# The first norm of a decoder layer: three token blocks ahead of any split, the other six in two groups of three

## The chip, the cores and the metric

The kernel runs on one core of a Trainium2 chip. The metric is the device time of one execution in microseconds. A core has a matrix engine (TensorE, PE in the rows, with its weight loads as PEld), a vector engine (VectorE, DVE), a scalar engine for activations, copies and casts (ScalarE, ACT), GpSimd (POOL), and SyncE (SP), which here issues DMA transfers. Each engine takes its instructions in order and waits on semaphores for the others.

## The reference

One step of a hybrid decoder layer for 1056 tokens (1024 of a prompt and 32 of eight samples) of width 1024, in float32. Cut to what the change touches:

```python
def _rmsnorm(x, g):
    y = x * lax.rsqrt(jnp.mean(x * x, axis=-1, keepdims=True) + EPS) * g
    return y

h = _rmsnorm(x, norm1)
z = h @ w_in                     # columns: hq, hf, hi, hog, aq, ak, av, iq, ik, iw, ga, gb
hq, hf, hi, hog, aq, ak, av, iq, ik, iw, ga, gb = jnp.split(z, offs, axis=-1)
# HGRN2 recurrence over hq, hf, hi; its output is normed and multiplied with silu(hog)
# sparse attention over aq, ak, av with an indexer iq, ik, iw
# merge with sigmoid(ga), sigmoid(gb), projection w_o, residual
# second norm, squared-ReLU MLP, residual, final norm
```

## The kernel before

The kernel is one program of some 31,000 instructions. It is written as a sequence of tile operations, and the build (`schedule_with_timeline_sim=True`, near the end of the file) plans the order on each engine from a simulated timeline: among instructions that are ready the one that stands earlier in the text goes first, and those written under `tc.high_priority()` go ahead of others. So the text sets which work is preferred, and data dependencies set what can't be overtaken.

**Split products.** A float32 product is made of three: each operand is split into a high part, rounded to the type `F32R`, and a low part, the rest. The high part is a cast on ScalarE, the low part a subtraction on VectorE. `wload` (L142 to L150) loads 128 columns of a weight matrix (512 KB) from SyncE into the raw tile `wr`, of which there is one buffer, and splits it into `wh` and `wl`, of which there are two each. In `wload` the split has high priority. `gemm3` (L152) does the three products for each of eight pieces of 128 rows, and `proj` and `proj_two` run it over three column pieces of 352 tokens (`CUTS`), so that the first piece needs token blocks 0 to 2, the second blocks 2 to 5, the third blocks 5 to 8.

**The first norm** (L208 to L240). Tokens come in nine blocks of 128 (the last has 32). `GROUPS` takes them as 0, 1, 2, (3, 4), (5, 6), (7, 8). For a group:

- each block is loaded (`xt`, SyncE) and squared with a row sum into `ss` (L225, ScalarE);
- `rstd_of` (L183) makes 1/sqrt: a step on VectorE (L186), a square root on ScalarE (L187), a reciprocal and three small steps on VectorE (L188 to L192);
- for each block the product `ht` = x * rstd * g (L234, VectorE), eight transposes on TensorE into a two-bank tile of PSUM (L238; `ps_s` has two buffers), the high split `hh` (L239, ScalarE) and the low split `hl` (L240, VectorE), both of which read that tile.

Once the group that holds block 2 (`FIRST_W`) is squared, the first two weight tiles are loaded: `whi` (input) and `whog` (output gate) of head 0. After the last group its rstd gives `zc` (L244) and from it `idr`, an identity matrix, with which the raw tokens are transposed too (`xTp`, L253, TensorE), copied (L255) and stored for the residual. These transposes and the later work are free to be planned among the products.

**After it** comes the loop over four heads of the HGRN2 branch (L393). For head 0 the products `whi` and `whog` run piece by piece in turn (`proj_two`, L406): `ev_i` copies, `ev_og` (L396) takes the sigmoid of the gate on ScalarE and multiplies. Square root and sigmoid use different tables of ScalarE, and going from one to the other shows as an ACT_TABLE_LOAD.

Of the kernel before, what the change touches and what calls it, by code (L numbers as in the profile page):

```python
# [10 lines left out]
F32 = mybir.dt.float32  # L11
# [3 lines left out]
AF = mybir.ActivationFunctionType  # L15
ALU = mybir.AluOpType
# [3 lines left out]
D = 1024  # L20
# [15 lines left out]
N_UNITS = 26  # L36
DOTS_S, DOTS_L = "sstts", "sstsstss"
CUTS = (0, 352, 704, 1056)

GROUPS, FIRST_W = ((0,), (1,), (2,), (3, 4), (5, 6), (7, 8)), 2  # L40

TH, TC = 528, 264
ORDER = ("P1", "P2", "P6", "P5", "P7", "P4", "P3")
# [18 lines left out]
C_HQ, C_HF, C_HI, C_HOG, C_AQ, C_AK, C_AV, C_IQ, C_IK, C_GA, C_GB = (  # L62
    0, 512, 1024, 1536, 2048, 2560, 3072, 3584, 4096, 4168, 5192)
# [37 lines left out]
def hybrid_step(ctx: ExitStack, tc, x_prompt, x_sample, cache_k, cache_v, cache_idx_k, state_hgrn,  # L101
# [3 lines left out]
    nc = tc.nc  # L105
    dbg = dbg or {}

    cst = ctx.enter_context(tc.tile_pool(name="cst", bufs=1))
# [30 lines left out]
    hl = big.tile([128, 8, T], F32R, name="hl", tag="hl")  # L139


    def wload(rows, c0, nk, m, name):  # L142
        raw = wp.tile([128, nk, m], F32, name=name + "r", tag="wr", bufs=1)
        nc.sync.dma_start(raw, rows[:, c0:c0 + m].rearrange("(k p) m -> p k m", p=128))
        wh = wp.tile([128, nk, m], F32R, name=name + "h", tag="wh", bufs=2)
        wl = wp.tile([128, nk, m], F32R, name=name + "l", tag="wl", bufs=2)
        with tc.high_priority():
            nc.scalar.copy(wh, raw)
            nc.vector.tensor_tensor(wl, raw, wh.bitcast(F32), op=ALU.subtract)
        return wh, wl  # L150

# [49 lines left out]
    g1 = U.get([128, 1024], F32, "g1")  # L201
    nc.scalar.dma_start(g1, bass.AP(tensor=norm1.tensor, offset=norm1.offset, ap=[[0, 128], [1, D]]))

    def tok(tb):
        n = 128 if tb < 8 else NS
        return n, slice(tb * 128, tb * 128 + n)
# [3 lines left out]
    nc.scalar.activation(zc, ones[:, 0:1], AF.Sqrt)  # L210
    hr = Ring(U, 6)
    xts = []
    first_w = None
    for grp in GROUPS:
        ss = sm.tile([128, 3], F32, name="ssx", tag="ssx", bufs=3)
        if 8 in grp:
            nc.vector.memset(ss, 1.0)
        hts = []
        for a, tb in enumerate(grp):
            n, cs = tok(tb)  # L220
            xt = U.get([128, 1024], F32, "xt")
            src = x_prompt[0, cs, :] if tb < 8 else x_sample.rearrange("s q d -> (s q) d")
            nc.sync.dma_start(xt[:n], src)
            ht = hr.get([128, 1024], F32, "ht")
            nc.scalar.activation(ht[:n], xt[:n], AF.Square, accum_out=ss[:n, a:a + 1])  # L225
            xts.append(xt)
            hts.append(ht)
        if not first_w and grp[-1] >= FIRST_W:
            first_w = [wload(w_in[0], C_HI, 8, 128, "whi"), wload(w_in[0], C_HOG, 8, 128, "whog")]
        rs = rstd_of(ss[:, :len(grp)], len(grp), 1.0 / D, "rsx")  # L230
        for a, tb in enumerate(grp):
            n, cs = tok(tb)
            ht = hts[a]
            nc.vector.scalar_tensor_tensor(ht[:n], xts[tb][:n], rs[:n, a:a + 1], g1[:n], op0=ALU.mult, op1=ALU.mult)  # L234
            pst = ps_s("hTp")
            pv = pst.rearrange("p a (b c) -> p (a b) c", c=128)
            for k in range(8):
                nc.tensor.transpose(pv[:, k, :n], ht[:n, k * 128:(k + 1) * 128], ident[:n, :n])  # L238
            nc.scalar.copy(hh[:, :, cs], pv[:, :, :n])  # L239
            nc.vector.tensor_tensor(hl[:, :, cs], pv[:, :, :n], hh[:, :, cs].bitcast(F32), op=ALU.subtract)  # L240
    U.put(g1)
    hr.close()

# [149 lines left out]
    for h in range(4):  # L393
        vT = U.get([128, T], F32, "vT")

        def ev_og(ps, sl, c):  # L396
            sg_ = sm.tile([128, CH], F32, name="sgo", tag="c352", bufs=2)
            sg_ = sg_[:, :sl.stop - sl.start]
            nc.scalar.activation(sg_, ps, AF.Sigmoid)
            nc.vector.tensor_tensor(sil[:, sl], ps, sg_, op=ALU.mult)  # L400

        def ev_i(ps, sl, c):
# [1134 lines left out]
```

## Time and profile before

| | us |
|---|---|
| median of 3 runs | 1807.02 |
| the three runs | 1801.29, 1807.02, 1813.28 |
| the profiled execution | 1804.69 |
| its span, first to last instruction | 1803.0 |
| TensorE busy in the span | 1718.2 |
| VectorE busy | 1222.6 |
| ScalarE busy | 867.4 |

The profile is one execution taken by the hardware profiler. A timeline row has the start and the length of an instruction (or of several alike, "x8"), its engine, line, operation, output tile and inputs, and in brackets how long the engine was idle before it and which instruction it then waited for. A row of stretches has how long each engine was busy in a stretch. Matmuls overlap, so that the spacing of their starts says more than the length of one.

### The profile page before, as it was taken

To read this page: it belongs to the slowest core of one execution; us is meant where nothing else is said; L and a number is where in the kernel's file an instruction comes from. 1 tells how busy PE (TensorE), PEld (TensorE's weight loads), DVE (VectorE), ACT (ScalarE), POOL (GpSimd) and SP (SyncE) were. 2 spreads that over 40 slices of the span, in tenths; PEclk is the share of its full clock that TensorE was granted. 3 is DMA by queue.
4 is the path that set the end of the run, shared out by engine and by line. 5 is a ranking of instruction groups with operands and counts; after the bars stand their busy time and mean duration, and the time that the engine had idled before them with its cause. 6 is when DMAs were issued, how large, how long until landed. Compare 5 with 4: busy or idle time off the path is not lost.

```text
span 1803.0 us, 30879 instructions
## 1 busy us (share of the span) xinstructions
PE 1718.2 (95%) x11980; PEld 1656.2 (92%) x11980; DVE 1222.6 (68%) x2767; ACT 867.4 (48%) x1645; POOL 216.7 (12%) x244
## 2 busy tenths in 40 slices
PE   6999999999999999979999999999999999999887
PEld 6999999999999998877899998999999899999867
DVE  7275585745799897965747569777677866566535
ACT  6456465334578833234724455444344644444412
POOL 1100000023000015740100230000000000000110
PEclk9999999999999999999999999999999999999998
DMA  5411111231223234552543243444334877676763
GB/s 167 132 49 48 49 56 48 61 94 34 84 68 96 77 95 130 172 180 66 162 143 108 95 132 99 145 151 160 132 132 156 275 178 182 174 185 166 171 155 115
DMA packets 162706, 221.92 MB, mean 123 GB/s; under 512 B 12096, under 2 KB 117856, under 8 KB 162560
## 3 DMA queue, kind: packets, MB, share of 16 engines
q1 hardware_dynamic: 137472, 148.60, 26.4%
q0 software_dynamic: 18032, 62.18, 13.4%
q10 hardware_dynamic: 7056, 9.18, 1.4%
q8 instruction: 94, 1.54, 0.4%
q14 instruction: 52, 0.43, 0.1%
HBM read 140.31 MB, written 76.77 MB: 120 GB/s over the span
## 4 chain that ended last, share of the span: by engine, by line
PE 38%; DMA 9%; issue 8%; DVE 4%; ACT 3%; POOL 2%; DVEq 0%; SPq 0%; POOLq 0%; ACTq 0%
PE pua L1336 13%; PE puc L1336 7%; PE pub L1336 3%; DMA qb<-q_d 2%; PE po L158 2%; PE po L157 2%; PE po L156 2%; DMA h2a<-hc_d 2%; DMA wdr<-in_w_down_dram 1%; POOL qb L924 1%; DMA h2b<-hc_d 1%; DMA wbsg<-sg_d 1%; DVE pr L923 1%; PE wbp L156 1%; PE wbp L157 1%
## 5 line engine op out<-in xcount | busy, mean ns | idle before, releaser
L1336 PE MATMUL pua<-h2P,wP 128*128 128x264 f32 x1248 | 196.1, 285 | 3.5 <-ACT uu L1398 3.1
L1336 PE MATMUL pua<-h2a,wP 128*128 128x264 f32 x960 | 161.7, 287 | 13.6 <-ACT uu L1398 10.6
L1336 PEld LDWEIGHTS pua<-h2P,wP 128*128 128x128 f32 x1248 | 170.4, 189 | 4.5 <-ACT uu L1398 4.0
L1336 PEld LDWEIGHTS pua<-h2a,wP 128*128 128x128 f32 x960 | 134.6, 189 | 18.9 <-ACT uu L1398 14.8
L1398 ACT COPY uu<-pua 128x264 f32<-128x264 f32 x192 | 72.0, 378 | 133.5 <-PE pua L1336 127.4
L156 PE MATMUL wgt<-hh,wgth 128*128 128x352 f32 x384 | 126.1, 328 | 0.0
L158 PE MATMUL wgt<-hh,wgtl 128*128 128x352 f32 x384 | 125.1, 326 | 0.0
L157 PE MATMUL wgt<-hl,wgth 128*128 128x352 f32 x384 | 124.6, 324 | 0.0
L1336 PE MATMUL pua<-h2b,wP 128*128 128x264 f32 x672 | 118.4, 285 | 0.0
L1336 PE MATMUL puc<-h2P,wP 128*128 128x264 f32 x720 | 111.0, 284 | 0.6 <-DVE hd L1402 0.6
L1440 POOL DMA_DIRECT2D x_d<-hd x32 | 27.9, 873 | 612.6 <-ACT wP L1302 359.5
L1336 PEld LDWEIGHTS puc<-h2P,wP 128*128 128x128 f32 x720 | 97.1, 188 | 0.8 <-DVE hd L1402 0.8
L777 ACT ACTIVATE jkA<-sc,bstg 128x1024 bf16<-128x1024 bf16 (+5 forms) x93 | 87.1, 936 | 21.3 <-DVE bstg L796 6.0
L1336 PEld LDWEIGHTS pua<-h2b,wP 128*128 128x128 f32 x672 | 96.8, 189 | 0.1
L772 DVE TENSOR_SCALAR_CACHE_REDUCE jkD<-sc,bstg 128x768 bf16<-128x768 f32 (+3 forms) x96 | 84.4, 879 | 0.9
L1303 DVE TENSOR_TENSOR wP<-w1r,wP 128x512 fp32r<-128x512 f32 (+2 forms) x96 | 62.8, 655 | 28.8 <-ACT wP L1302 28.0
L1302 ACT CAST wP<-w1r 128x512 fp32r<-128x512 f32 (+2 forms) x96 | 57.0, 595 | 46.7 <-PE puc L1336 28.1
L156 PEld LDWEIGHTS wgt<-hh,wgth 128*128 128x128 f32 x384 | 72.2, 188 | 2.0 <-issue 1.0
L157 PEld LDWEIGHTS wgt<-hl,wgth 128*128 128x128 f32 x384 | 72.2, 188 | 1.2 <-issue 0.5
L158 PEld LDWEIGHTS wgt<-hh,wgtl 128*128 128x128 f32 x384 | 72.2, 188 | 1.2 <-issue 0.6
L1336 PE MATMUL puc<-h2a,wP 128*128 128x264 f32 x384 | 70.6, 286 | 0.9 <-DVE hd L1408 0.9
L158 PE MATMUL po<-mh,wol 128*128 128x352 f32 x192 | 62.2, 324 | 0.0
(788 smaller groups left out, 5071.2 us busy)
## 6 DMA issues: line engine op xcount, KB each, us to landing
x_d<-hd POOLq DMA_DIRECT2D x32, 528.0 KB
hc_d<-hd SPq DMA_DIRECT2D x56, 264.0 KB, 2.8
h2P<-hc_d SPq DMA_DIRECT2D x45, 264.0 KB, 3.7
sg_d<-gst ACTq DMA_DIRECT2D x48, 176.0 KB, 2.0
h2a<-hc_d SPq DMA_DIRECT2D x32, 264.0 KB, 2.8
wgtr<-in_w_in_dram SPq DMA_DIRECT2D x16, 512.0 KB, 3.9
qb<-q_d POOLq DMA_DIRECT2D x16, 512.0 KB
w1r<-in_w_up_dram SPq DMA_DIRECT2D x16, 512.0 KB, 3.9
```

The costliest lines, as they stand in the source:

```text
L156: nc.tensor.matmul(ps, wh, xh, start=(k == 0), stop=False)
L157: nc.tensor.matmul(ps, wh, xl, start=False, stop=False)
L158: nc.tensor.matmul(ps, wl, xh, start=False, stop=(k == n - 1))
L772: nc.vector.tensor_scalar(jkD[:, 0, :L], SC[i], s if isinstance(s, float) else s[:, a:a + 1], 0.0, op0=op, op1=ALU.add, accum_out=out[:, a ...
L777: nc.scalar.activation(jkA[:, 0, :(i + 1) * 128], src(i), AF.Sign, bias=thr[:, a:a + 1], accum_out=cnt[:, a:a + 1])
L923: nc.vector.tensor_tensor(pr, kp[:, 0:1, :].to_broadcast([128, 2, 512]), qb, op=ALU.mult)
L924: nc.gpsimd.tensor_tensor(qb, kp[:, 1:2, :].to_broadcast([128, 2, 512]), qb, op=ALU.mult)
L1302: nc.scalar.copy(w[:, 0, :n], src)
L1303: nc.vector.tensor_tensor(w[:, 1, :n], src, w[:, 0, :n].bitcast(F32), op=ALU.subtract)
L1336: nc.tensor.matmul(ps, w[:, a, k], x[:, b, sl], start=(q in "P1P2P5" and k == n_ == 0), stop=(k == k1 - k0 - 1 and n_ == 2), skip_group_ch ...
L1398: nc.scalar.copy(uu[c][:, {"P1": u1, "P6": 1, "P7": 2}[q]], ps)
L1440: nc.gpsimd.dma_start(x1_d[2 * i + e], hd[j][e], accum_op=ALU.add)
```

## The change

The first three blocks are normed (`norm`) one by one, before any of them is transposed and split (`turn`). A column of ones, `one`, is computed from the rstd of block 2 (the maximum with 1, then the minimum with 1, is 1 for every number) and is the scale with which ScalarE writes the high splits of blocks 0 and 1 and of the `whi` weights; these therefore follow the third root. The other six blocks go in two groups of three. The second group's factor `inv` (1/1024 for every number) is computed from a column of the high split of block 3, so that its root follows that split. The splits of the first two weights have no high priority any more; `whi` is loaded after block 0 is turned and `whog` after blocks 3 to 5 are normed. The scale `onel`, a one from the last group's rstd, makes the first sigmoid follow the last root. In `wload` the cast of the high part, for all weights, is written as an activation (Copy with a scale) instead of a copy.

```diff
--- before.py
+++ after.py
@@ -37,8 +37,6 @@
 DOTS_S, DOTS_L = "sstts", "sstsstss"
 CUTS = (0, 352, 704, 1056)
 
-GROUPS, FIRST_W = ((0,), (1,), (2,), (3, 4), (5, 6), (7, 8)), 2
-
 TH, TC = 528, 264
 ORDER = ("P1", "P2", "P6", "P5", "P7", "P4", "P3")
 
@@ -139,13 +137,13 @@
     hl = big.tile([128, 8, T], F32R, name="hl", tag="hl")
 
 
-    def wload(rows, c0, nk, m, name):
+    def wload(rows, c0, nk, m, name, late=None):
         raw = wp.tile([128, nk, m], F32, name=name + "r", tag="wr", bufs=1)
         nc.sync.dma_start(raw, rows[:, c0:c0 + m].rearrange("(k p) m -> p k m", p=128))
         wh = wp.tile([128, nk, m], F32R, name=name + "h", tag="wh", bufs=2)
         wl = wp.tile([128, nk, m], F32R, name=name + "l", tag="wl", bufs=2)
-        with tc.high_priority():
-            nc.scalar.copy(wh, raw)
+        with tc.high_priority() if late is None else ExitStack():
+            nc.scalar.activation(wh, raw, AF.Copy, scale=1.0 if late is None else late)
             nc.vector.tensor_tensor(wl, raw, wh.bitcast(F32), op=ALU.subtract)
         return wh, wl
 
@@ -210,8 +208,9 @@
     nc.scalar.activation(zc, ones[:, 0:1], AF.Sqrt)
     hr = Ring(U, 6)
     xts = []
-    first_w = None
-    for grp in GROUPS:
+
+    def norm(grp, inv=1.0 / D):
+
         ss = sm.tile([128, 3], F32, name="ssx", tag="ssx", bufs=3)
         if 8 in grp:
             nc.vector.memset(ss, 1.0)
@@ -225,19 +224,47 @@
             nc.scalar.activation(ht[:n], xt[:n], AF.Square, accum_out=ss[:n, a:a + 1])
             xts.append(xt)
             hts.append(ht)
-        if not first_w and grp[-1] >= FIRST_W:
-            first_w = [wload(w_in[0], C_HI, 8, 128, "whi"), wload(w_in[0], C_HOG, 8, 128, "whog")]
-        rs = rstd_of(ss[:, :len(grp)], len(grp), 1.0 / D, "rsx")
+        rs = rstd_of(ss[:, :len(grp)], len(grp), inv, "rsx")
         for a, tb in enumerate(grp):
             n, cs = tok(tb)
-            ht = hts[a]
-            nc.vector.scalar_tensor_tensor(ht[:n], xts[tb][:n], rs[:n, a:a + 1], g1[:n], op0=ALU.mult, op1=ALU.mult)
+            nc.vector.scalar_tensor_tensor(hts[a][:n], xts[tb][:n], rs[:n, a:a + 1], g1[:n], op0=ALU.mult,
+                                           op1=ALU.mult)
+        return grp, hts, rs
+
+    def turn(grp, hts, rs):
+
+        for ht, tb in zip(hts, grp):
+            n, cs = tok(tb)
             pst = ps_s("hTp")
             pv = pst.rearrange("p a (b c) -> p (a b) c", c=128)
             for k in range(8):
                 nc.tensor.transpose(pv[:, k, :n], ht[:n, k * 128:(k + 1) * 128], ident[:n, :n])
-            nc.scalar.copy(hh[:, :, cs], pv[:, :, :n])
+            nc.scalar.activation(hh[:, :, cs], pv[:, :, :n], AF.Copy, scale=one[:, 0:1] if tb < 2 else 1.0)
             nc.vector.tensor_tensor(hl[:, :, cs], pv[:, :, :n], hh[:, :, cs].bitcast(F32), op=ALU.subtract)
+
+
+    normed = [norm((tb,)) for tb in range(3)]
+
+    one = cst.tile([128, 1], F32, name="one")
+    nc.vector.tensor_scalar(one, normed[2][2][:, 0:1], 1.0, 1.0, op0=ALU.max, op1=ALU.min)
+    turn(*normed[0])
+    first_w = [wload(w_in[0], C_HI, 8, 128, "whi", late=one)]
+    turn(*normed[1])
+    turn(*normed[2])
+    inv = 1.0 / D
+    for grp in ((3, 4, 5), (6, 7, 8)):
+        normed = norm(grp, inv)
+        if len(first_w) == 1:
+            first_w.append(wload(w_in[0], C_HOG, 8, 128, "whog", late=1.0))
+        turn(*normed)
+
+        inv = cst.tile([128, 1], F32, name=f"inv{grp[0]}")
+        nc.vector.tensor_scalar(inv, hh[:, 7, tok(grp[0])[1]][:, 127:128].bitcast(F32), 1.0 / D, 1.0 / D,
+                                op0=ALU.max, op1=ALU.min)
+    rs = normed[2]
+
+    onel = cst.tile([128, 1], F32, name="onel")
+    nc.vector.tensor_scalar(onel, rs[:, 0:1], 1.0, 1.0, op0=ALU.max, op1=ALU.min)
     U.put(g1)
     hr.close()
 
@@ -396,7 +423,7 @@
         def ev_og(ps, sl, c):
             sg_ = sm.tile([128, CH], F32, name="sgo", tag="c352", bufs=2)
             sg_ = sg_[:, :sl.stop - sl.start]
-            nc.scalar.activation(sg_, ps, AF.Sigmoid)
+            nc.scalar.activation(sg_, ps, AF.Sigmoid, scale=onel if h == c == 0 else 1.0)
             nc.vector.tensor_tensor(sil[:, sl], ps, sg_, op=ALU.mult)
 
         def ev_i(ps, sl, c):
```

## Rows read from the trace of the kernel before

**Rows 1.** The page's busy times: us, share of the span, instructions.
```profile
PE 1718.2 (95%) x11980; PEld 1656.2 (92%) x11980; DVE 1222.6 (68%) x2767; ACT 867.4 (48%) x1645; POOL 216.7 (12%) x244
```

**Rows 2.** Busy times by stretches: length, engines, granted clock (PEclk), DMA share, GB/s.
```profile
0.00:50.00 50.00, 34.44 (x219) 32.75 (x220) 33.66 (x123) 32.40 (x54) 9.61 (x24) 1.00 0.52 164
...
800.00:850.00 50.00, 39.94 (x216) 29.99 (x215) 22.84 (x77) 20.13 (x39) 3.13 (x6) 0.90 0.22 68
```

**Rows 3.** The same view, of a stretch soon after the start.
```profile
25.40:30.40 5.00, 5.00 (x34) 5.00 (x32) 4.89 (x9) 1.02 (x1) 0.00 (x0) 1.00 0.38 103
```

**Rows 4.** TensorE's timeline of the start: start, length, line, operation, count [idle before].
```profile
9.87 1.94 PE L238 MATMUL hTp<-ident,ht 128*128 128x128 f32 x8 [9.87 <-DVE rsx L186]
...
18.44 1.94 PE L238 MATMUL hTp<-ident,ht 128*128 128x128 f32 x8 [4.30 <-DVE rsx L186]
...
21.40 1.94 PE L238 MATMUL hTp<-ident,ht 128*128 128x128 f32 x8 [1.02 <-DVE ht L234]
...
25.62 0.32 PE L158 MATMUL whi<-hh,whil 128*128 128x352 f32 x1
...
25.77 0.32 PE L156 MATMUL whi<-hh,whih 128*128 128x352 f32 x1
...
34.54 1.04 PE L253 MATMUL xTp<-idr,xt 128*128 128x128 f32 x8
...
36.65 0.41 PE L156 MATMUL whi<-hh,whih 128*128 128x352 f32 x1
```

**Rows 5.** ScalarE's timeline of the start.
```profile
9.93 1.04 ACT L225 ACTIVATE ht<-xt 128x1024 f32<-128x1024 f32 x1
...
11.84 1.01 ACT L239 CAST hh<-hTp 128x1024 fp32r<-128x1024 f32 x1 [0.78 <-PE hTp L238]
...
12.75 1.05 ACT L148 CAST whih<-whir 128x1024 fp32r<-128x1024 f32 x1
...
13.70 0.20 ACT L187 ACTIVATE rsx<-rsx 128x1 f32<-128x1 f32 x1
...
24.29 0.21 ACT L187 ACTIVATE rsx<-rsx 128x2 f32<-128x2 f32 x1
...
33.58 1.28 ACT L399 ACT_TABLE_LOAD   x1
...
34.88 0.46 ACT L399 ACTIVATE sgo<-whog 128x352 f32<-128x352 f32 x1
```

**Rows 6.** VectorE's timeline of the start.
```profile
10.05 0.16 DVE L188 RECIPROCAL rsx<-rsx 128x1 f32<-128x1 f32 x1 [0.27 <-ACT rsx L187]
...
10.83 1.28 DVE L234 SCALAR_TENSOR_TENSOR ht<-xt,rsx,g 128x1024 f32<-128x1024 f32 x1
...
12.03 0.15 DVE L186 TENSOR_SCALAR rsx<-ssx 128x1 f32<-128x1 f32 x1
...
14.03 1.22 DVE L149 TENSOR_TENSOR whil<-whir,whih 128x1024 fp32r<-128x1024 f32 x1
...
17.01 1.28 DVE L234 SCALAR_TENSOR_TENSOR ht<-xt,rsx,g 128x1024 f32<-128x1024 f32 x1
...
26.03 1.22 DVE L149 TENSOR_TENSOR whogl<-whogr,whogh 128x1024 fp32r<-128x1024 f32 x1
...
35.11 1.20 DVE L240 TENSOR_TENSOR hl<-hTp,hh 128x1024 fp32r<-128x1024 f32 x1
```

**Rows 7.** SyncE's timeline; the DMA view to 75 us (KB, us to landing).
```profile
15.27 0.38 SPq L144 DMA_DIRECT2D whogr<-in_w_in_dram  x1
...
whogr<-in_w_in_dram SPq DMA_DIRECT2D x2, 512.0 KB, 4.6
```

**Rows 8.** ScalarE's instructions by line and shape: count, busy us, mean ns of one.
```profile
L1258 ACT ACTIVATE x<-x,g 128x1056 f32<-128x1056 f32 x7 | 8.2, 1178 | 11.3 <-DMA x_d<-x 11.3
...
L459 ACT ACTIVATE eb<-b 128x1056 f32<-128x1056 f32 x4 | 4.4, 1088 | 4.1 <-DVE b L442 4.1
...
L1454 ACT CAST h2b<-h2b 128x1056 fp32r<-128x1056 f32 x4 | 4.3, 1076 | 4.4 <-DMA h2b<-hid_d 4.0 <-PE puc L1336 0.4
```

## The prediction

> **What bounds the kernel now.** I read the page's busy times first: TensorE is busy 1718.2 us, 95% of the span of 1803.0 [rows 1], so the end is set by when TensorE starts and by the holes in its stream, 84.8 us in all. Second, the busy times by stretches: the first 50 us hold 15.56 us of that (50.00 - 34.44); the largest later one, 800 to 850 us, holds 10.06 [rows 2]. The change touches the first. In a full stretch soon after the start TensorE and VectorE have no rest while ScalarE works 1.02 of 5.00 us [rows 3].
>
> Third, TensorE's timeline of the start. The eight transposes of token block 0 begin at 9.87; before those of block 2, at 18.44, TensorE is idle for 4.3 us, and before those of block 3, at 21.40, for 1.0. From there on nothing is missing [rows 3, 4]. The first 9.87 us wait for the first tokens, their square and root; a better order could win the 4.3 + 1.0 = 5.3 us behind it and no more.
>
> Fourth, who made the 4.3 us hole. Block 2's square starts at 9.93 and VectorE's step after it (L186) at 12.03, so its root could run at 12.2. ScalarE was by then in the high splits of block 0 (11.84) and of the first weights (12.75), and the root came at 13.70 [rows 5]. VectorE then took the weights' low split (14.03), which has priority, and others, and block 2's product `ht` came at 17.01 [rows 6]. Splits stand ahead of the norm that feeds the next transposes.
>
> **The change part by part.**
>
> *The third root ahead of the splits.* `one` is made from block 2's rstd and scales the high splits of blocks 0 and 1 and of the first weights, so none of the three can start before that root. The new times are my working from the durations in these rows. Root at 12.2. In block 1 the reciprocal began at 10.05 and the product at 10.83, so 0.8 from the end of the root to rstd: 13.2. `one` costs what L186 costs, 0.15. Product of block 2: 13.4 to 14.7 (1.28) [rows 6]. High split of block 0: 13.4 to 14.5 (1.01 and the pointer, below), where it began at 11.84 [rows 5]: 1.6 us late. Its low split: 14.7 to 15.9 (1.2, as at 35.11). Here comes the next limit: `ps_s` has two buffers, and block 0's is free only after its low split, so the transposes of block 2 start at 15.9 and not at 14.7; before it was 18.44 [rows 4]. They end at 17.9 (1.94), the high split at 18.9, the low split at 20.1. The first product of `whi` can start at 18.9, its stream at 20.1; before, the full stream began at 21.4. So with the same three blocks transposed, TensorE becomes full **1.3 to 2.5 us earlier**. I take 1.7, near the lower end: block 3, which could fill the time between, is not ready by then (next part).
>
> *Blocks 3 to 8 in threes.* Two roots instead of three; one group's five small VectorE steps of some 0.15 go, 0.8 us. But no product of blocks 3, 4 and 5 starts before all three squares are done (1.04 each), and ScalarE has the three splits from 13.4 to 16.6 and block 2's from 17.9 to 18.9, so the last square ends near 20 and block 3's product starts near 21. The second group also waits, by `inv`, for block 3's high split. From 21 VectorE needs 3 x 1.28 for the products, 3 x 1.2 for the low splits and 1.22 for the gate weights until block 5 is split: 8.7 us, at 29.7, or 31 with the steps of the next group between. Before, VectorE began block 6's split, the one after block 5's, at 35.11 [rows 6], and the second column piece of `whi`, which needs block 5, began at 36.65 [rows 4]. That is 4 to 5 us of slack; I cost the part at nothing. If that cover were gone, each us late would stand in TensorE's stream.
>
> *The first weights lose priority.* The raw tile `wr` has one buffer, so the gate weights' transfer starts when the first weights' low split ends: issued at 15.27, as that split ended at 15.25 [rows 6, 7]. Now their high split runs 14.5 to 15.6 behind `one` and the low split 15.9 to 17.1: the transfer starts 1.8 us later. On SyncE's queue only later loads of the same tile stand behind it, for which TensorE has both `whi` and `whog` to do first. It lands 4.6 us after its issue [rows 7], at 21.7. The gate weights were split at 27.25 before (26.03 and 1.22); by my times TensorE wants them at about 28. Cost nothing if planned in time; the other case is a rival.
>
> *Added instructions.* Four VectorE steps of one column (`one`, `onel`, two `inv`), 0.15 each: 0.6 us. Four ScalarE instructions take a column as scale; at 1056 columns that form took 1178 ns against 1088 without, 0.09 each, 0.4 us in all [rows 8]. Those on the path are in the times above. The cast in `wload` becomes an ACTIVATE, 65 times over the kernel: 1088 against 1076, 0.01 each [rows 8], beside a TensorE stream during which ScalarE mostly waits [rows 3]. Bounds: 0, and 0.8 us if all 65 stood on the path. I take 0.
>
> *The first sigmoid after the last root.* The last root of this stage is at 24.29 and the sigmoid's table load at 33.58 [rows 5]: the order asked for is there already, so nothing is gained. What it guards against is a gate product that overtakes the root, two more loads. Their price by the rows: the load takes 1.28 us and the sigmoid starts at 34.88, 0.02 after its end, so 2.6 us of ScalarE for two. The Trainium skill (ScalarE: Activation LUTs, "What ACT_TABLE_LOAD costs") puts a drain of about 1.38 us on top of each load; no such gap is in the row, and by the page the two would cost 5.3 us.
>
> **The sum.** -1.7 us and nothing added. The profiled execution took 1804.69 us (span 1803.0 and 1.7 around it): 1803.0. By the median shown, 1807.02, it is 1805.3. I take the middle, 1804.
>
> **Rivals.**
> 1. *No gain.* The start moves but a hole opens behind it in the same stage. For it: VectorE is full there [rows 3]. Against: the slack above. 1806.
> 2. *Slower: the gate weights come last.* Without priority the first weights' low split may be planned after block 2's (20.1 to 21.3); the transfer then lands at 25.9, and the gate weights' splits, 1.05 and 1.22 at the least, can queue behind the three products (3.8 us): ready at up to 32. TensorE by then has had the first piece of `whi` (24 products, one each 0.16 [rows 4], 3.8 us and some at half rate) and three blocks of transposes (3.1), to about 28.5. It decides from the point where that split ends after 28.5; price 3.5 - 1.7 = 1.8 us: 1808.
> 3. *The clock comes up late.* Eight transposes took 1.94 us at 18.44 and 21.40 and 1.04 at 34.54 [rows 4]: half the rate, as 1.2 to 2.4 GHz, although the column of granted clock reads 1.00 [rows 2, 3]. Products come each 0.16 from 25.6 on, after TensorE had been full since 21.4. If the new start has holes and the rate rises only at the old time, the first piece of `whi` runs at half rate: 24 x 0.16 = 3.8, less 1.7: 1808. The Trainium skill (TensorE: Matmul & The Clock Gate, Part 1) has the clock gated to half until sustained activity releases it; by that rule the lost time moves along with the start of the full stream, and the rival needs holes in it.
> 4. *The order elsewhere shifts.* Each engine's order is planned from a simulated timeline over the whole kernel; a start moved by 2 us and other costs for 65 casts can reorder far away. Behind the start lie 69 us of holes, in pieces of up to 10 us, that one at a clock of 0.90 [rows 2]. One such piece filled, or one more made, is some 10 us either way: 1794 or 1814. To pass 1%, 18 us, it takes two.
>
> **How the numbers follow.** Forecast (a gain of 1 to 4 us) 0.42; no gain 0.16; gate weights late 0.12; clock late 0.10; order elsewhere better 0.10, worse 0.10. The three runs shown spread over 12 us, so a median of a few may be off by 4. The forecast's own range with that is 1799 to 1809; up to both arms of the last rival it becomes 1795 to 1813. About 1% is what a measurement of this kernel tells from no change, and only the last rival reaches it, with about half of each arm. Faster by over 1%: 0.06; within: 0.88; slower: 0.06.
>
> **What the profile after would show.** The root of block 2 ahead of every high split, near 12.2; its transposes near 15.9, behind block 0's low split; TensorE full from about 19 to 20; the gate weights' transfer issued near 17; no table load between the first root and the sigmoid. I am wrong if block 2's transposes stay past 18, if holes of over 2 us follow in the first 50 us, or if TensorE's busy time in stretches behind 100 us differs from that of before by several us.

## Result, and the profile after

The changed kernel took 1819.03 us (median of 20 runs, 1806.83 to 1827.84), the kernel before 1810.28 (20 runs, 1795.64 to 1823.43): a ratio of 1.0051 with a 95% interval of 1.0029 to 1.0072, so 5 to 13 us slower, by the ratio 9.2. That is outside the predicted range. The profiled execution of after took 1826.81 us (span 1825.1), one of its longer ones; what follows compares single steps, not spans.

Busy time of after in two stretches (columns: start:end, its length, then busy time and count of PE, PEld, DVE, ACT and POOL, granted clock, DMA share, GB/s):

```profile
0.00:50.00 50.00, 26.55 (x137) 23.79 (x138) 33.80 (x121) 27.80 (x44) 6.96 (x21) 0.93 0.41 129
50.00:100.00 50.00, 50.00 (x336) 49.37 (x335) 10.10 (x14) 21.85 (x38) 7.98 (x9) 1.00 0.45 135
```

TensorE is busy 26.55 us in the first 50, where it was 34.44 [rows 2]; from 50 on it is full. So 7.9 us are lost as idle time in the stage that the change touches; work done at half rate adds to that, and isn't seen in busy time. A better measure is the start of the first product `whf` (the forget gate), for by then TensorE has done the same 369 instructions in every kernel (but for the extra transposes of e8 and e10, and for nine small instructions that e9 does later, below). The products of that name in before, and then in after (count, shortest/median/longest ns, start of the first and of the last):

```profile
L156 PE MATMUL whf<-hh,whfh x96: 319/322/495, 72.0 to 299.1; 128*128 128x352 f32 x96
```

```profile
L154 PE MATMUL whf<-hh,whfh x96: 319/322/495, 83.8 to 317.4; 128*128 128x352 f32 x96
```

The first comes 11.8 us later. I call this time **the mark**: 72.0 before, 83.8 after.

Where the 11.8 us arise, on TensorE's timeline of after (start, length, operation, idle time before it and what ended that):

```profile
12.38 1.97 PE L241 MATMUL hTp<-ident,ht 128*128 128x128 f32 x8 [0.37 <-DVE rsx L184]
18.35 1.97 PE L241 MATMUL hTp<-ident,ht 128*128 128x128 f32 x8 [4.01 <-DVE hl L243]
23.15 0.66 PE L154 MATMUL whi<-hh,whih 128*128 128x352 f32 x1 [2.83 <-ACT hh L242]
24.41 0.66 PE L155 MATMUL whi<-hl,whih 128*128 128x352 f32 x1 [0.60 <-DVE hl L243]
24.86 0.49 PE L156 MATMUL whi<-hh,whil 128*128 128x352 f32 x1
25.16 0.49 PE L154 MATMUL whi<-hh,whih 128*128 128x352 f32 x1
...
29.52 0.32 PE L154 MATMUL whi<-hh,whih 128*128 128x352 f32 x1
29.67 0.32 PE L155 MATMUL whi<-hl,whih 128*128 128x352 f32 x1
...
31.42 1.91 PE L241 MATMUL hTp<-ident,ht 128*128 128x128 f32 x16
...
36.03 1.03 PE L241 MATMUL hTp<-ident,ht 128*128 128x128 f32 x8
38.66 1.07 PE L241 MATMUL hTp<-ident,ht 128*128 128x128 f32 x8 [1.60 <-DVE ht L230]
42.20 1.15 PE L241 MATMUL hTp<-ident,ht 128*128 128x128 f32 x8 [2.48 <-DVE scr L346]
44.28 1.03 PE L241 MATMUL hTp<-ident,ht 32*128 32x32 f32 x8 [0.94 <-DVE inv L262]
45.25 1.97 PE L280 MATMUL xTp<-idr,xt 128*128 128x128 f32 x8
47.78 1.12 PE L280 MATMUL xTp<-idr,xt 128*128 128x128 f32 x4 [0.57 <-ACT xT L282]
48.55 0.64 PE L154 MATMUL whi<-hh,whih 128*128 128x352 f32 x1
```

Block 2's transposes start at 18.35, where they started before, 18.44 [rows 4]. Products start at 23.15. The first column pieces of `whi` and `whog`, with the transposes of blocks 3 and 4, last to 36. Then TensorE runs dry, with holes of 1.60, 2.48, 0.94 and 0.57 us and little between them, and the second piece of `whi` starts at 48.55; it was 36.65 [rows 4]. From here after lags by 11.9, which is the mark's 11.8.

What held that piece? Not its operands alone. A column piece is written to a buffer of PSUM, and there are two of these for `whi` and `whog`. The second piece of `whi` needs the one that the first piece of `whi` leaves when ScalarE copies it into `vT` (`ev_i`). `vT` is a tile handed out anew, and for head 0 it is the memory of block 0's raw tokens; it can't be written before these are transposed (`xTp`), which needs `idr`, which needs `zc`, which needs the rstd of the **last** group. In the variant e7 (below) the wait stands in a row of ScalarE as such:

```profile
43.07 0.45 ACT L430 COPY vT<-whi 128x352 f32<-128x352 f32 x1 [0.27 <-PE xTp L280]
```

ScalarE's and VectorE's timelines of after, from the root of block 2 on:

```profile
12.41 0.20 ACT L185 ACTIVATE rsx<-rsx 128x1 f32<-128x1 f32 x1 [0.54 <-DVE rsx L184]
13.61 1.06 ACT L224 ACTIVATE ht<-xt 128x1024 f32<-128x1024 f32 x1 [0.99 <-DMA xt<-in_x_prompt_dram]
14.88 1.06 ACT L224 ACTIVATE ht<-xt 128x1024 f32<-128x1024 f32 x1
15.94 1.09 ACT L242 ACTIVATE hh<-hTp,one 128x1024 fp32r<-128x1024 f32 x1
...
24.03 0.19 ACT L185 ACTIVATE rsx<-rsx 128x3 f32<-128x3 f32 x1
...
32.49 1.94 ACT L242 ACTIVATE hh<-hTp 128x1024 fp32r<-128x1024 f32 x2 [7.32 <-PE hTp L241]
36.19 0.20 ACT L185 ACTIVATE rsx<-rsx 128x3 f32<-128x3 f32 x1 [1.76 <-DVE rsx L184]
...
47.63 0.46 ACT L430 COPY vT<-whi 128x352 f32<-128x352 f32 x1
```

```profile
26.34 3.67 DVE L230 SCALAR_TENSOR_TENSOR ht<-xt,rsx,g 128x1024 f32<-128x1024 f32 x3
33.55 1.22 DVE L243 TENSOR_TENSOR hl<-hTp,hh 128x1024 fp32r<-128x1024 f32 x1 [3.54 <-ACT hh L242]
34.69 0.14 DVE L262 TENSOR_SCALAR inv<-hh 128x1 f32<-128x1 f32 x1
34.75 1.21 DVE L243 TENSOR_TENSOR hl<-hTp,hh 128x1024 fp32r<-128x1024 f32 x1
35.88 0.22 DVE L184 TENSOR_SCALAR rsx<-ssx,inv 128x3 f32<-128x3 f32 x1
...
37.23 3.67 DVE L230 SCALAR_TENSOR_TENSOR ht<-xt,rsx,g 128x1024 f32<-128x1024 f32 x3
...
40.88 0.13 DVE L271 TENSOR_SCALAR zc<-rsx 128x1 f32<-128x1 f32 x1
...
44.13 0.31 DVE L273 TENSOR_SCALAR idr<-ident,zc 128x128 f32<-128x128 f32 x1
```

In before the chain has these rows, two of VectorE and one of ScalarE:

```profile
30.07 2.47 DVE L234 SCALAR_TENSOR_TENSOR ht<-xt,rsx,g 128x1024 f32<-128x1024 f32 x2
32.47 0.13 DVE L244 TENSOR_SCALAR zc<-rsx 128x1 f32<-128x1 f32 x1
```

```profile
35.70 0.47 ACT L403 COPY vT<-whi 128x352 f32<-128x352 f32 x1
```

So in before it read: last root 24.29 [rows 5], last two products 30.07, `zc` 32.47, `xTp` 34.54 [rows 4], `vT` 35.70, second piece 36.65. After: 36.19, 37.23, 40.88, 45.25, 47.63, 48.55. The lag grows in four steps: the last products start 7.2 us later; three in a row before `zc` in place of two, 1.25; from `zc` to `xTp` 4.37 in place of 2.07, since `idr` stands behind low splits on VectorE, 2.3; from `xTp` to `vT` 2.4 in place of 1.2. Sum 11.9.

The root is at 36.19 because its first step (L184) reads `inv`, `inv` reads the high split of block 3 (32.49; in before 23.38), and the transposes for that (31.42) stand on TensorE behind the whole first piece of `whi`; two low splits (33.55 and 34.75) then stand ahead of `inv` and of L184 on VectorE. The transposes stand there since block 3's product ran only at 26.34.

### The profile page after: what moved, and what is told of

The parts are those of the page before. It is cut to its first block, busy times and chain, and to the rows that moved or that the text cites. A ratio compares the mean times of both kernels' runs of the same rounds, so it can differ in the third digit from the quotient of the medians.

```text
span 1825.1 us, 30879 instructions
## 1 busy us (share of the span) xinstructions
PE 1732.0 (95%) x11980; PEld 1669.6 (91%) x11980; DVE 1222.9 (67%) x2766; ACT 869.4 (48%) x1644; POOL 217.0 (12%) x244
## 3 DMA queue, kind: packets, MB, share of 16 engines
q0 software_dynamic: 18032, 62.18, 13.4%
## 4 chain that ended last, share of the span: by engine, by line
PE 35%; issue 13%; DMA 7%; DVE 4%; POOL 3%; ACT 2%; SPq 0%; DVEq 0%; POOLq 0%; ACTq 0%
PE pua L1363 12%; PE puc L1363 6%; PE pub L1363 3%; DMA qb<-q_d 2%; PE po L156 2%; PE po L155 2%; PE po L154 2%; POOL qb L951 1%; DMA wdr<-in_w_down_dram 1%; DMA h2P<-hc_d 1%; POOL x_d L1467 1%; PE wbp L154 1%; PE wbp L155 1%; PE wbp L156 1%; PE wap L154 1%
## 5 line engine op out<-in xcount | busy, mean ns | idle before, releaser
L1330 DVE TENSOR_TENSOR wP<-w1r,wP 128x512 fp32r<-128x512 f32 (+2 forms) x96 | 62.5, 652 | 29.7 <-ACT wP L1329 29.0
L1363 PE MATMUL puc<-h2b,wP 128*128 128x264 f32 x336 | 60.3, 287 | 2.3 <-DVE hd L1429 2.3
```

Source lines behind the costliest of these rows:

```text
L1330: nc.vector.tensor_tensor(w[:, 1, :n], src, w[:, 0, :n].bitcast(F32), op=ALU.subtract)
L1363: nc.tensor.matmul(ps, w[:, a, k], x[:, b, sl], start=(q in "P1P2P5" and k == n_ == 0), stop=(k == k1 - k0 - 1 and n_ == 2), skip_group_ch ...
```

## The experiments

The theory of the expectations is this chain: the late last root, through `zc`, the raw transposes and the tile of `vT`, sets when TensorE's stream goes on. The rivals are that late splits or products of blocks 3 to 8 hold the stream up by themselves, that the clock does, or that the casts and the sigmoid do. Each variant ran ten times, beside 25 to 31 runs of before. The edits are cut to their main lines. Times of single steps in us (`whq`, the query product, comes between the second piece and the mark), each from one profiled execution:

| | high split of block 0 | transposes of block 2 | last root | `zc` | second piece | `whq` | mark | ratio to before [95%] |
|---|---|---|---|---|---|---|---|---|
| before | 11.84 | 18.44 | 24.29 | 32.47 | 36.65 | 58.0 | 72.0 | |
| after | 15.94 | 18.35 | 36.19 | 40.88 | 48.55 | 69.8 | 83.8 | 1.0051 [1.0029, 1.0072] |
| e1_no_inv | 15.14 | 17.54 | 24.27 | 33.58 | 40.42 | 61.8 | 76.0 | 0.9980 [0.9956, 1.0005] |
| e2_pairs | 14.62 | 17.04 | 24.77 | 32.99 | 39.59 | 60.2 | 74.4 | 1.0000 [0.9974, 1.0026] |
| e3_threes_alone | 11.78 | 18.37 | 27.61 | 33.27 | 41.06 | 61.2 | 75.5 | 1.0029 [0.9999, 1.0060] |
| e4_raw_early | 16.24 | 18.65 | 37.81 | 14.85 | 41.13 | 64.9 | 76.5 | 1.0002 [0.9976, 1.0029] |
| e5_before_raw_early | 11.78 | 18.43 | 28.10 | 16.95 | 36.88 | 59.4 | 71.0 | 1.0004 [0.9972, 1.0036] |
| e6_casts_sigmoid | 12.07 | 18.67 | 24.54 | 32.70 | 37.75 | 59.1 | 73.0 | 1.0032 [0.9992, 1.0072] |
| e7_squares_after | 13.57 | 15.99 | 28.80 | 36.70 | 43.62 | 65.7 | 79.7 | 1.0020 [0.9988, 1.0052] |
| e8_warm | 15.46 | 18.39 | 32.95 | 37.65 | 45.31 | 66.4 | 80.5 | 1.0046 [1.0016, 1.0076] |
| e9_own_tile | 15.02 | 17.42 | 35.43 | 40.13 | 37.42 | 65.1 | 79.3 | 1.0059 [1.0035, 1.0082] |
| e10_both | 13.51 | 17.94 | 25.92 | 16.45 | 36.13 | 58.2 | 69.9 | 0.9972 [0.9945, 0.9999] |
| e11_again | 14.95 | 17.35 | 35.25 | 39.95 | 47.61 | 68.9 | 82.9 | 1.0050 [1.0017, 1.0083] |

### e1_no_inv: after without `inv`

```diff
-        inv = cst.tile([128, 1], F32, name=f"inv{grp[0]}")
-        nc.vector.tensor_scalar(inv, hh[:, 7, tok(grp[0])[1]][:, 127:128].bitcast(F32), 1.0 / D, 1.0 / D,
-                                op0=ALU.max, op1=ALU.min)
```

> The changed kernel without the wait `inv`: the second group of three may take its root before block 3 is split. Mark: the start of the first product of `whq`, 57.98 us in the kernel before and 69.80 in the changed one. Theory (the last root came too late, 36.19 against 24.29, and the transposes of the raw tokens, the tile of `vT` and so the second column piece hang on it): the last root is back at 24 to 27, the mark at 60 to 62, total time +0 to +4 us over the kernel before. Rival A (the splits of blocks 0 and 1 and of the first weights held behind the third root cost the time): the mark stays at 67 to 70, total +8 to +11. Rival B (the time is lost elsewhere, by another order): the mark tells nothing, total stays at +8 to +11 although the mark comes back.

ScalarE's timeline of this kernel:

```profile
23.23 0.19 ACT L185 ACTIVATE rsx<-rsx 128x3 f32<-128x3 f32 x1
...
24.27 0.19 ACT L185 ACTIVATE rsx<-rsx 128x3 f32<-128x3 f32 x1
30.99 1.94 ACT L242 ACTIVATE hh<-hTp 128x1024 fp32r<-128x1024 f32 x2 [6.54 <-PE hTp L241]
```

Block 3's high split is nearly as late as in after (30.99 against 32.49), but the last root no longer waits for it, 24.27. The mark falls from 83.8 to 76.0 and the whole loss in total time is gone, 1807.81 us against 1810.59 for before. So the one-column instruction `inv` is what makes the change slow: 12.8 us between the two ratios (0.71% of 1810), of which 7.8 are seen at the mark.

### e2_pairs and e3_threes_alone: the two halves of the change

e2 is e1 with pairs in place of threes; e3 is before with threes and `inv`, without the early norms.

```diff
-    for grp in ((3, 4, 5), (6, 7, 8)):
+    for grp in ((3, 4), (5, 6), (7, 8)):
```

```diff
-GROUPS, FIRST_W = ((0,), (1,), (2,), (3, 4), (5, 6), (7, 8)), 2
+GROUPS, FIRST_W = ((0,), (1,), (2,), (3, 4, 5), (6, 7, 8)), 2
```

> The changed kernel with the old pairs (3, 4), (5, 6), (7, 8) and without `inv`: the first part of the change, the late splits and the late sigmoid alone. Theory: the mark (first product of `whq`) at 59 to 61, total +0 to +3 us over the kernel before; what is left is the later and slower start of the stream. Rival A: mark 67 to 70, total +8 to +11. If threes alone cost time too, this mark lies 1 us or more ahead of that of the kernel without `inv`.

> The kernel before with the groups (3, 4, 5) and (6, 7, 8) and with `inv`, nothing else: the second part of the change alone; splits keep their priority and wait for no root. Theory: the last root moves from 24.29 to 33 or later, the mark (first product of `whq`) from 57.98 to 65 to 68, total +6 to +10 us over the kernel before. Rival A: mark 57 to 59, total within 2 us of the kernel before.

Alone, the early norms (in e2 with the late splits of the weights and the late sigmoid) cost 2.4 us at the mark and nothing in the time; the threes with `inv` cost 3.5, and in the time 0.29% with an interval that just reaches no change. Early norms and threes without `inv` (e1) cost 4.0. All together cost 11.8, twice the 5.9 of the two halves. The reason is in the rows: in e3 block 3 is split at 23.25, as before, and `inv` costs the last root only 3.3 us. Only early norms and threes together push block 3 behind the first products (its high split is at 30.99 in e1, but at 23.86 in e2, with pairs), and only then does `inv` wait for something late. My expectation for e3 (65 to 68 for `whq`) took `inv` to be as dear there; it was 61.2.

e2 also bears on the first half of the prediction: block 2's transposes start 1.4 us earlier than in before, and TensorE is not full earlier for it, since those of block 3 come no sooner (21.67 against 21.40 [rows 4]) and the last two products run at 30.53 (before 30.07).

### e4_raw_early and e5_before_raw_early: `zc` off the last root

e4 is after with `zc` made from `one`; e5 is before with `zc` made from the rstd of block 2.

```diff
-    nc.vector.tensor_scalar(zc, rs[:, 0:1], 0.0, None, op0=ALU.mult)
+    nc.vector.tensor_scalar(zc, one, 0.0, None, op0=ALU.mult)
```

> The changed kernel with `zc` taken from `one` (the third root) in place of the last root: the raw tokens may be transposed early, the last root stays held by `inv`. Theory (the late root costs because the raw transposes and the tile of `vT` wait for it): TensorE has no hole of over 1 us between 25 and 50, the mark (first product of `whq`) at 58 to 62, total -1 to +4 us against the kernel before, although the last root stays at 33 or later. Rival C (the late root costs because the low splits of blocks 5 to 8 come late, whatever fills the time): mark 65 to 69. Rival A: the stream of products still starts at 23 to 25 and the mark stays at 67 to 70.

> The kernel before with `zc` taken from the third root in place of the last: the raw tokens may be transposed as soon as TensorE has a hole. Mark from now on: the first product of `whf`, by which all raw transposes are done in every variant but a few (72.01 us in the kernel before, 83.84 in the changed one, 76.0 without `inv`, 76.5 with early raw transposes). Theory (a hole is free for raw transposes, and their copies cost ScalarE time that its splits want): holes before 25 us shrink by 1 to 2 us, the mark at 70 to 73, total -3 to +2 us. Rival (raw transposes early always help, as they only fill holes): mark 68 to 70.

In e4 the last root is even later than in after, 37.81, the last three products start at 38.86, and yet the mark is 76.5: 7.3 of the 11.8 us are back, and the time is that of before. So the late root, and the late splits that follow it, are not what costs most; it is that raw transposes hang on it. They hang on it in two ways. The second piece starts at 41.13 and its second product, behind block 5's low split (42.51), at 44.62, where after has 48.99: some 4 of the 7.3 us. And by then 44 of the 72 raw transposes are done, in holes of TensorE from 15 us on, where after has done 12; that is the rest. `whq` came later than I expected, 64.9, for the raw transposes now run ahead of it; at the mark, when they are done in every kernel, the gain shows. In before the same edit gains 1.0 at the mark, no more than two profiles of one kernel differ by (e11), and nothing in the time, and the second piece starts at 36.88 and no sooner: there `zc` came in time.

### e9_own_tile: tiles of their own for `vT` and `sil`

After, with `vT` and `sil` of head 0 taken as tiles of their own ahead of the mask `mk_u`; `zc` still hangs on the last root.

```diff
+    own0 = [U.get([128, T], F32, n) for n in ("vT", "sil")]
     mk_u = U.get([128, T], I32, "mk_u")
-        vT = U.get([128, T], F32, "vT")
+        vT = U.get([128, T], F32, "vT") if h else own0[0]
-            sil = U.get([128, T], F32, "sil")
+            sil = own0[1]
```

> The changed kernel with tiles of their own, free from the start, for `vT` and `sil` of head 0; in it they are the tiles that held the raw tokens of block 0 and their transposed copy. Last root, `inv`, groups and `zc` are as in the changed kernel. Theory (the second column piece of `whi` waits for the copy of the first into `vT`, and this for the raw transposes of block 0, and these for `zc` at 40.88): the copy into `vT` at 32 to 35 in place of 47.63, the second piece of `whi` ahead of the raw transposes, its start at 43 to 44 (behind the low split of block 5 at 42.15) in place of 48.55, mark (first product of `whf`) 78 to 80 against 83.84, total -3 to -6 us against the changed kernel. Rival C (the low splits set the time whatever the tiles): second piece starts earlier but the third waits for block 8, mark 82 to 84.

First ScalarE's, then TensorE's timeline of this kernel:

```profile
29.89 0.45 ACT L431 COPY vT<-whi 128x352 f32<-128x352 f32 x1 [5.65 <-PE whi L156]
...
35.43 0.20 ACT L185 ACTIVATE rsx<-rsx 128x3 f32<-128x3 f32 x1 [1.76 <-DVE rsx L184]
```

```profile
37.42 0.43 PE L154 MATMUL whi<-hh,whih 128*128 128x352 f32 x1 [1.11 <-ACT hh L242]
37.90 1.07 PE L241 MATMUL hTp<-ident,ht 128*128 128x128 f32 x8
41.45 1.09 PE L241 MATMUL hTp<-ident,ht 128*128 128x128 f32 x8 [2.48 <-DVE hl L243]
42.29 0.49 PE L155 MATMUL whi<-hl,whih 128*128 128x352 f32 x1
```

The copy into `vT` is at 29.89, right behind its products and ahead of `zc` (40.13); in after it was at 47.63. That shows the chain's link through the tile. The second piece starts 11.1 us earlier than in after, but with one product: the next product needs the low split of block 5, which is late as well (two low splits at 40.19, 2.33 us), and the stream goes on at 42.29. So two waits stood one behind the other, and taking away the first uncovers the second; the mark gains 4.5 us (3.6 against e11), of which some 0.6 is no gain, as the eight raw transposes of the last, small block run only behind it. The total did not follow: I expected 3 to 6 us less than after, and it is 1.0059.

### e6_casts_sigmoid: casts as activations, and the sigmoid's scale

Before, with both casts (`wh` and `hh`) written as activations, and with `onel`.

```diff
-            nc.scalar.copy(wh, raw)
+            nc.scalar.activation(wh, raw, AF.Copy, scale=1.0)
-            nc.scalar.activation(sg_, ps, AF.Sigmoid)
+            nc.scalar.activation(sg_, ps, AF.Sigmoid, scale=onel if h == c == 0 else 1.0)
```

> The kernel before with the casts of `wload` and of the high splits written as activations (scale 1.0) and with the first sigmoid behind the last root (`onel`); norm, groups and priorities as before. Theory (these two parts cost nothing by themselves): mark (first product of `whf`) 71.5 to 72.5, total within 3 us of the kernel before. Rival B (a different planned order far behind the start moves the total): mark unchanged, total off by 5 us or more either way.

The mark is 73.0, 1.0 late, again no more than two profiles of one kernel differ by. The time is 1.0032, 5.8 us where I expected 3 at most, with an interval that reaches from no change to 0.7%. So this run doesn't clear these parts, nor does it exclude its rival, another order far behind the start; e1, which holds them too, is not slower than before.

### e7_squares_after: the split ahead of the squares

e2 with the squares of blocks 3 and 4 scaled by `one`, so that they can't be planned ahead of the splits, and with `one` made ahead of block 2's product.

```diff
-            nc.scalar.activation(ht[:n], xt[:n], AF.Square, accum_out=ss[:n, a:a + 1])
+            nc.scalar.activation(ht[:n], xt[:n], AF.Square, scale=one[:n, 0:1] if tb in (3, 4) else 1.0,
+                                 accum_out=ss[:n, a:a + 1])
```

> The kernel with the first part alone (old pairs, no `inv`), with two edits: `one` is computed ahead of block 2's product, and the squares of blocks 3 and 4 take `one` as scale, so that they can't stand ahead of the splits of blocks 0 and 1 on ScalarE. Without these edits: high split of block 0 at 14.62, transposes of block 2 at 17.04, stream from 24, mark (first product of `whf`) 74.4. Theory (what kept block 2 late in the changed kernel was squares planned ahead of the splits): high split of block 0 at 13.4 to 13.7, transposes of block 2 at 16, mark at 72 to 73.5, total -4 to +1 us against the kernel before. Rival (block 2 comes earlier, but the squares that were put off make the pair 3, 4 later by as much): transposes of block 2 at 16, mark 74 to 76.

Here a step of the prediction comes true: the high split of block 0 starts at 13.57 and block 2's transposes at 15.99 (13.4 and 15.9 were forecast). And the kernel gets worse than e2, mark 79.7 against 74.4. ScalarE's timeline shows the price:

```profile
15.62 1.14 ACT L226 ACTIVATE ht<-xt,one 128x1024 f32<-128x1024 f32 x1
...
16.75 1.10 ACT L247 ACTIVATE hh<-hTp,one 128x1024 fp32r<-128x1024 f32 x1
17.75 1.14 ACT L226 ACTIVATE ht<-xt,one 128x1024 f32<-128x1024 f32 x1
...
23.94 0.19 ACT L185 ACTIVATE rsx<-rsx 128x2 f32<-128x2 f32 x1
```

The square of block 3 comes behind block 0's split and that of block 4 behind block 1's. Then the squares of blocks 5 to 8 and block 2's split stand ahead of the root of blocks 3 and 4, which comes at 23.94; in e2 it was at 17.66. I had expected a mark of 72 to 73.5 and the rival said 74 to 76, so both missed. In these rows ScalarE is the queue of this stage: what one block gains in it, the next pays.

### e8_warm: TensorE kept busy

After with 110 transposes of the identity into a tile that nobody reads.

```diff
+    warm = ps_t("warm")
+    for k in range(110):
+        nc.tensor.transpose(warm[:, (k % 4) * 128:(k % 4 + 1) * 128], ident, ident)
```

> The changed kernel with 110 extra transposes of the identity into a spare PSUM tile nobody reads, planned into TensorE's holes of the first 20 us, so that TensorE is busy before the first products of `whi`. Theory (16 of the 24 products of the first piece came each 0.29 us instead of 0.16, which is 2.1 us, and block 3's transposes stand behind them): products 0.16 apart from the start, transposes of block 3 earlier by 2 us or more, mark (first product of `whf`) 80 to 82 against 83.84, total -1 to -4 us against the changed kernel. Rival (the slow products are hidden, as what follows waits for VectorE anyway): products at full rate, mark 83 to 85.

The first piece of `whi` now runs 0.16 apart from its third product on, and the mark is 80.5, 3.3 earlier than after's. The time shows none of it: 1.0046. Half rate is part of the loss at the mark, and its cure alone did not move the total.

### e10_both and e11_again

e10 puts three things on **before**: `zc` from the rstd of block 2, own tiles for `vT` and `sil`, and 80 transposes that nobody reads. e11 is after once more, beside e9 and e10.

> The kernel before with `zc` from the third root, own tiles for `vT` and `sil` of head 0, and 80 extra transposes of the identity that keep TensorE busy to about 14 us. It asks whether the start can be made faster than before at all. Theory (TensorE is free of waits from about 17 us, at full rate, and raw transposes fill what is left): mark (first product of `whf`) 67 to 70 against 72.01, total -1 to -6 us against the kernel before, which may be too little to tell. Rival (ScalarE, whose copies of the raw transposes now stand among its splits, is the bound of the start): mark 71 to 74.

> The changed kernel as it is, beside the two others on the same chip: how far the mark and the total of one kernel repeat. All theories: mark (first product of `whf`) 83 to 85, last root 36 to 37, total +6 to +12 us over the kernel before. If the mark differs by over 2 us, single profiles can't carry the comparisons made with it.

e10 has the earliest mark, 69.9, and 1801.39 us against 1807.98: 0.9972 with an interval that ends just under 1. It is faster than after (e11, beside it); against before, in one of eleven such comparisons, it stands at the edge of what the runs tell. Which of the three edits does it, they don't separate. In its first 50 us, the extra transposes included:

```profile
0.00:50.00 50.00, 42.52 (x317) 41.17 (x318) 34.43 (x124) 33.87 (x58) 12.59 (x28) 1.00 0.64 200
```

e11 repeats after: mark 82.9 and last root 35.25, each some 0.1 to 0.8 below what I had expected, ratio 1.0050. So the marks of one program differ by 0.9 us in these two executions, and differences of that size between kernels tell nothing.

## Why the prediction was wrong

**The step that failed** is "I cost the part at nothing", on the threes and `inv`. I had written that the second group waits by `inv` for block 3's high split, and then took as slack the distance from the end of block 5's split (29.7 to 31) to the split after it in before (35.11); block 5's own was done there by 34.23. I followed the wait to the operands of the second piece and not to the other thing that hangs on the last group's rstd: `zc`, `idr`, the raw transposes, and through a reused tile the PSUM buffer of that same piece. In before this chain came just in time: `xTp` 34.54, the copy into `vT` from 35.70 to 36.17, second piece 36.65. It did not hold the piece (e5), but half a us was left at its end, and not 4 to 5. I took the raw transposes for filler that is "free to be planned among the products". The term was 0; `inv` alone measured 7.8 of the 11.8 us at the mark (e1), and what e1 keeps, threes and early norms with the rest, 4.0.

**Its times were off too.** Block 3's product was forecast near 21 and ran at 26.34; block 5's split was to be done by 31, and its low split ran at 40.95. Two of the signs of being wrong that I had named stood in the profile: block 2's transposes past 18 (18.35) and a hole of over 2 us in the first 50 (2.48). I had the three squares end near 20. ScalarE took all the others as well (18.97 to 24) ahead of the group's root.

**The third root ahead of the splits** (a gain of 1.7). The root came as forecast, 12.2 and 12.41. The next line failed: high split of block 0 at 13.4. It ran at 15.94, because ScalarE had the squares of blocks 3 and 4 first, for the first of which it also waited on a DMA for 0.99 us. In e11, without that wait, it ran at 14.95, so the order makes most of the delay. The plan is made from a simulated timeline, and an instruction that waits in the chip holds up all behind it. The two-buffer limit that I found is there: block 2's transposes were released by `hl` (L243), at 18.35 and not 15.9. e7 shows that reaching 15.9 would have won nothing: the term was not only mis-sized; earlier transposes of three blocks don't fill TensorE if the next group is later. I had read ScalarE's load from a stretch behind the start, where it mostly waits [rows 3], and did not write out its queue between 12 and 24 us, where it has no rest.

**The first weights.** The cost of nothing held: the gate weights' transfer was issued as the first weights' low split ended, at 19.45 (near 17 was forecast), and their split was done at 26.4, ahead of TensorE's need at 30.46. The second rival (gate weights last) did not happen.

**Casts, columns as scale, sigmoid.** In the rows of after a high split with a column took 1.09 to 1.14 us against 1.01 to 1.05 without, as costed. No table load lies between the first root and the sigmoid. The sum of these at nothing was not refuted and, by e6, not proved.

**The rivals.** The third (the clock) happened as it was put, holes in the new start: 16 of 24 products of the first piece were 0.29 apart, 24.86 to 29.52, against 0.16, which is 2.1 us, and the rate fell once more after the holes at 38 to 44 (eight raw transposes in 1.97 at 45.25, against 1.04 [rows 4]). I had put the price at 3.8, less a gain that did not come; keeping TensorE busy gave back 3.3 of the 11.8 at the mark (e8). The first rival named a hole in the same stage, as it came, but priced it at no more than the gain. None of the rivals held the chain; the one that I should have had, "the second group's root waits for a split that TensorE has to make room for", was one sentence away from my text.

**Shown and open.** Shown: without `inv` the loss is gone, in the time too (e1); at the mark `inv` costs that much only with the early norms beside it (e3, whose time lies between and doesn't decide). With the raw transposes off the last root, 7.3 us at the mark and the loss in time are gone (e4). The tile of `vT` is one link between them and the second piece (e9), worth 3 to 4 us at the mark and nothing that can be seen in the time. For `zc` later than 33 the mark follows it, 42.2 to 43.0 us behind it in e1, e3, e7, e8, after and e11. Open: why the total doesn't follow the mark more closely, as in e8 and e9. From the mark to the last `whf` product TensorE took 227.1 us in before and 233.6 in after, most of the difference in two stretches of heads 1 to 3 that lie at a lower granted clock, here in after:

```profile
167.00:199.00 32.00, 32.00 (x204) 30.35 (x203) 28.44 (x52) 21.01 (x23) 1.46 (x2) 0.91 0.21 67
255.00:298.00 43.00, 43.00 (x288) 41.39 (x288) 28.85 (x53) 20.06 (x23) 2.36 (x3) 0.92 0.17 46
```

and the two that answer to them in before, at 1.00 (222 instructions of TensorE in the 32 us instead of 204, and 290 in 40 us where after took 43 for 288):

```profile
155.00:187.00 32.00, 32.00 (x222) 30.35 (x221) 29.11 (x53) 22.10 (x25) 1.46 (x2) 1.00 0.22 67
240.00:280.00 40.00, 40.00 (x290) 38.38 (x289) 28.93 (x53) 20.00 (x23) 2.36 (x3) 1.00 0.17 49
```

TensorE shows no idle time in either. e11 has the two stretches at 0.91 and 0.92 too, so they come again with this program. But they don't explain the total: in e9 the column reads 1.00 from 70 to 310, and e9 is as slow as after, while e2, with the column at 0.90 from 160 to 190 and 0.89 from 250 to 280, takes the time of before. Why that clock is lower was not settled.

Nor can the 9 us be added up from profiles. The profiled span of after is 22.1 us longer than that of before: 11.8 at the mark, 6.5 from there to the last `whf` product, 3.8 behind it. That of e11 is 14.1 longer: 10.9, 6.2 and -3.0. Each is one execution, and executions of one kernel spread by over 20 us. Whether my last rival, an effect far from the change, has a part in it, no run shows.

## What to carry to other kernels

A wait is followed to everything that hangs on the late value, not to the next consumer alone: here a constant made from the last root opened raw transposes, these a tile, and the tile a PSUM buffer that the main stream needed; what the allocation of tiles reuses is a dependency that the formulas don't show. Where an engine's order is planned, write out the whole queue of the busiest engine of the stage before costing an earlier start, as what one block gains there the next one loses. An artificial dependency that costs one column is priced by the time at which its input will come in the *new* order.

## What the runs showed of the hardware

The granted clock in the rows doesn't tell the rate at the start. In before eight transposes took 1.94 us while the column read 1.00 [rows 2 to 4], and so they do in after at 10.07; in e2, eight transposes took 1.94 as well, in a stretch (20 to 25 us) where the column read 0.50. The spacing of products is what to read: 0.29 or 0.16.

The table load for the sigmoid came at 40.80 and took 1.28 us, and the sigmoid ran at 42.10. The Trainium skill (ScalarE: Activation LUTs, "What ACT_TABLE_LOAD costs") adds a drain of about 1.38 us to each load. Neither this row nor that of before [rows 5] has one between the load and the instruction that needs it.
